# One-hot routing grids: two tokens interleaved instead of four

## The chip, the cores and the metric

The kernel runs on one core of a Trainium2 chip. The core has five engines: TensorE (matrix products, called PE in the profile, with its weight loads listed apart as PEld), VectorE (DVE), ScalarE (ACT), GpSimd (POOL) and SyncE (SP, which here only issues transfers). They run side by side and wait for each other on semaphores. The metric is the time of one execution on the device in microseconds (us). Before the change the median of three runs is 1775.51 us (1775.36 to 1782.84).

## The reference

The kernel computes one layer of a transformer-like backbone for 512 tokens of width 1024: a modulated norm, neighbourhood attention beside a gated MLP, a merge, and then a PEER feed-forward, a product-key lookup of experts. Only the last part matters here:

```
def block(xb):                                   # 128 tokens
    q = (xb @ wq).reshape(128, 8, 2, 128)        # 8 heads, two halves
    s = einsum('thpd,hpkd->thpk', q, sub_keys)
    s_top, i_top = top_k(s, 16)                  # 16 of 128 keys per half
    cand_s = s_top[:, :, 0, :, None] + s_top[:, :, 1, None, :]
    cand_i = i_top[:, :, 0, :, None] * 128 + i_top[:, :, 1, None, :]
    best_s, best_pos = top_k(cand_s, 16)         # 16 experts per head
    experts = take_along_axis(cand_i, best_pos)
    g = softmax(best_s)
    act = gelu(einsum('thkd,td->thk', expert_u[experts], xb))
    return einsum('thk,thkd->td', g * act, expert_v[experts])
```

Each token picks 8 x 16 = 128 of 16384 experts. An expert number is a pair (i, j), each from 0 to 127, and a gate g belongs to it.

## The kernel before, in words

The tokens are four tiles of 128. Three of them (`DT = 3`) take a dense path: all 16384 experts are evaluated as matrix products, in 128 blocks of 128 experts, and the experts that a token did not pick get the weight zero. The fourth tile gathers its experts' rows from memory (L992), on POOL's queue, with its arithmetic on DVE (L1002, L1007).

The dense path has three parts. **The u products** (`dense_u`, lines L82 to L88 and L846): for each of the 128 blocks, `uraw` is loaded, ACT rounds it to `uhi` (L82), DVE takes the rest as `ulo` (L83), PE makes 8 x 3 matmuls of 384 columns (three token tiles wide; L86, L87, L88), and ACT applies the gelu (L846). **The expansion** (L908 to L935): the sparse choice of each token is written out as a full 128 x 128 table of weights. **The v products** (`dense_v`, after L944): the table, read back from memory as `wr`, is multiplied with the gelu of u and gives the left side of the products with the rows of v, 512 columns each.

The change lies in the expansion. For a tile of 128 tokens, `columns` puts the choices on the partitions: `lt[0]` and `lt[1]` hold the row number i and the column number j of choice k (partition) of token t (column), `lt[2]` and `lt[3]` the gate as a large and a small fp16 part. The table of a token is then one product over the 128 choices: a one-hot matrix of j (128 choices x 128 keys), transposed, times a one-hot matrix of i that carries the gate. DVE builds these matrices for eight tokens at a time (`TB = 8`) with four instructions of 1024 fp16 elements per partition: `ea` (L915) and `eb` (L917) compare the numbers with a grid `iot` of 0 to 127, and `oa` (L921, twice) multiplies `ea` with the large and the small part of the gate. PE then makes two accumulating matmuls per token (L926): `eb` of the token is the stationary side, 128 x 128, and `oa` of the token the moving side, 128 columns. ACT copies the tables of four tokens out of PSUM (L927), and every 16 tokens a DMA of 1 MB takes them to memory (L935).

The tokens are not stored one behind the other. The grids have the shape (groups, 128, tokens of a group): neighbouring elements belong to neighbouring tokens, so that DVE's innermost run is over tokens. One token's row of 128 numbers therefore has a step as large as a group, and that is the step at which PE reads both sides of L926.

Per 8 tokens there are so 4 DVE instructions, 16 matmuls and 16 weight loads, 2 ACT copies; 48 such steps make three tiles, so 192 DVE instructions and 768 matmuls in all. The grids have 3 buffers each, the PSUM tiles 4. In the same loop stand the decoding of the next tile's choices (DVE and ACT, `decode`) and every second step one more block of the u products (`more_u`, `UR = 0.5`). The engines' final orders are set before the run by a scheduler, which interleaves these, so that PE goes through 48 of the small matmuls (three steps) in one go and then through some 48 wide ones of u products.

Of the kernel before, what the change touches and what calls it, by code (L numbers as in the profile page):

```python
# [12 lines left out]
HF = mybir.dt.float16  # L13
# [8 lines left out]
P = 128  # L22
# [25 lines left out]
def body(tc, A, out):  # L48
    nc = tc.nc
    pe, dve, act, pool, sp = nc.tensor, nc.vector, nc.scalar, nc.gpsimd, nc.sync  # L50
    es = ExitStack()

    def pool_(stack, name, side="left", bufs=1):
        return stack.enter_context(tc.tile_pool(name=name, bufs=bufs, side=side, reuse_waits="tile"))
# [6 lines left out]
    def ps(tag, shape=(P, 512)):  # L61

        t = psp.tile([P, 512], F32, name="ps" + tag, bufs=4 if tag == "m" else 2)
        n = int(np.prod(shape[1:]))
        v = t[:shape[0], :n]
        if len(shape) == 3:
            v = v.rearrange("p (a b) -> p a b", b=shape[2])
        return v
# [32 lines left out]
    ea = ExitStack()  # L101
# [3 lines left out]
    def t2(dt=F32):  # L105
        return tmp.tile([P, 512], dt, name="t2", bufs=8)
# [165 lines left out]
    eb = ExitStack()  # L272
# [79 lines left out]
    def proj_T(src, g, ins, n=4, sub=None, tags="mmmm"):  # L352

        o = [[ps(t, (P, w)) for t in tags] for _, _, w in ins[:1]]
        for _, _, w in ins[1:]:
            o.append([x[:, i, :] for x in [ps("x", (P, 2, w)) for _ in range(2)] for i in range(2)])
        last = 2 * n - 1
        for c, wh, wl in weights(src, g, n, sub=sub):
            for i, (rh, rl, _) in enumerate(ins):
                for b in range(4):  # L360
                    bs = slice(b * P, (b + 1) * P)
                    if i == 0:
                        mm3(o[i][b], wh[:, bs], wl[:, bs], rh[:, c, :], rl[:, c, :], c == 0, c == last)
                    else:
                        mm3(o[i][b], wh[:, bs], wl[:, bs], rh[:, c, :], rl[:, c, :], c == 0 and b % 2 == 0, c == last and b % 2 == 1, True)
        return o

    def proj_N(src, g, ins):

        o = [ps("m" if i < 4 else "x") for i in range(len(ins))]  # L370
        for c, wh, wl in weights(src, g):
            for i, (lh, ll, t) in enumerate(ins):
                ts = slice(t * P, (t + 1) * P)
                mm3(o[i], lh[:, c, ts], ll[:, c, ts], wh, wl, c == 0, c == 7)
        return o
# [56 lines left out]
    o = proj_N(A["w_in"], 2, lat_N + [(ch, cl, 0), (ch, cl, 1)])  # L432
    for t in range(NT):
        v = t2()
# [22 lines left out]
    for i in range(0, 8, 2):  # L457
        o = ps("xu"[i // 2 % 2], (P, 2, 256))
# [6 lines left out]
    o, = proj_T(A["w_in"], 0, lat_T)  # L465
# [133 lines left out]
    for n in range(2):  # L599
        o, = proj_T(A["w_in"], 7 + n, lat_T, tags=("mmmm", "uuxx")[n])  # L600
# [9 lines left out]
    for n in range(2):  # L610
        for nm, src in (("a", A["w_pa"]), ("b", A["w_pb"])):
            o, = proj_T(src, n, [(*y2[nm], S)], n=2, tags={"a": "mmmm", "b": "uuxx"}[nm])
# [40 lines left out]
    o = proj_N(A["w_out"], 0, [(m_h, m_l, t) for t in range(NT)])  # L653
# [6 lines left out]
    for p in range(2):  # L660
        o = [ps("m"), ps("m")]
# [12 lines left out]
    for p in range(2):  # L674
        if p == 0:
            o = [x[:, i] for x in [ps("x", (P, 2, 256)) for _ in range(2)] for i in range(2)]
        else:
            o = [ps("m", (P, 256)) for _ in range(4)]
# [63 lines left out]
    for g in range(4):  # L742
        if g > 0:
            o, = proj_T(A["wq"], g, [(h2h, h2l, S)], sub=pool)
# [6 lines left out]
        for t in range(NT):  # L751
            o = ps("x" if g < 3 else "m", (P, 4, P))
# [24 lines left out]
    rs = pool_(ro, "rs", "right", bufs=2)  # L777
    TB = 8
    ioa = pr.tile([P, 16, 16], BF, name="ioa")
    iot = rs.tile([P, P, 4], HF, name="iot", bufs=1)  # L780

    def decode(t, res):

# [52 lines left out]
    def more_u(n, sub):  # L836
        for _ in range(n):
            if us_done[0] < P:
                dense_u(us_done[0], sub)
                us_done[0] += 1  # L840
# [16 lines left out]
    def natural_h2():  # L857
        for hf in range(2):
            o = ps("x", (P, 4, P))
            for c in range(4):  # L860
                cc_ = hf * 4 + c
                hs = rs.tile([P, P], F32, name="hs", bufs=1)
                dve.tensor_tensor(hs, f(h2h[:, cc_, GT * P:]), f(h2l[:, cc_, GT * P:]), op=OP.add)
                pe.transpose(o[:, c, :], hs, ident)
            act.activation(h2n[:, hf * 512:(hf + 1) * 512], o.rearrange("p a b -> p (a b)"), AF.Copy)
# [5 lines left out]
    def start_route(t):  # L871
        res = []
        return res, decode(t, res)

    more_u(2, pool)
    pool.iota(ioa, pattern=[[1, 16], [0, 16]], base=0, channel_multiplier=0, allow_small_or_imprecise_dtypes=True)
    pool.iota(iot, pattern=[[1, P], [0, 4]], base=0, channel_multiplier=0, allow_small_or_imprecise_dtypes=True)
    more_u(U0 - 2, pool)
    res, gen = start_route(0)
    for _ in gen:  # L880
# [1 line left out]
    def columns(res):  # L882

        lt = []
        for n, v in enumerate(res):
            o = ps("x", (P, P))
            pe.transpose(o, v.rearrange("p h k -> p (h k)"), ident)
            c = rs.tile([P, P], HF, name="lt%d" % n)
            act.activation(c, o, AF.Copy, scale=1.0 if n < 2 else WS)
            lt.append(c)  # L890

        r = rs.tile([P, P], HF, name="lt3")
        dve.scalar_tensor_tensor(r, o, WS, c, op0=OP.mult, op1=OP.subtract)
        lt.append(r)
        return lt
# [3 lines left out]
    for t in range(DT):  # L899
        lt = lt_next  # L900
        if t == 1:
            natural_h2()
        res, gen = start_route(t + 1)
        for g in range(P // TG):
            stg = rs.tile([P, P, TG], F32, name="stg")
            for u in range(TG // TB):
                t0 = g * TG + u * TB

                def spread(v):

                    return v[:, t0:t0 + TB].rearrange("p (g o t) -> p g o t", g=2, o=1).to_broadcast([P, 2, P, 4])

                grid = iot.rearrange("p (o i) t -> p o i t", o=1).to_broadcast([P, 2, P, 4])
                ea_ = rs.tile([P, 2, P, 4], HF, name="ea", bufs=3)
                dve.tensor_tensor(ea_, spread(lt[0]), grid, op=OP.is_equal)  # L915
                eb_ = rs.tile([P, 2, P, 4], HF, name="eb", bufs=3)
                dve.tensor_tensor(eb_, spread(lt[1]), grid, op=OP.is_equal)  # L917
                oa = []
                for n in range(2):
                    oa.append(rs.tile([P, 2, P, 4], HF, name="oa%d" % n, bufs=3))  # L920
                    dve.tensor_tensor(oa[n], ea_, spread(lt[2 + n]), op=OP.mult)  # L921
                for v in range(2):
                    o = ps("m", (P, 4, P))
                    for x in range(4):
                        for n in range(2):
                            pe.matmul(o[:, x, :], eb_[:, v, :, x], oa[n][:, v, :, x], start=(n == 0), stop=(n == 1))  # L926
                    act.activation(stg[:, :, u * TB + v * 4:u * TB + v * 4 + 4], o.rearrange("p k i -> p i k"), AF.Copy, scale=1.0 / WS)  # L927
                if gen and next(gen, gen) is gen:
                    gen = None
                    if t + 1 < DT:  # L930
                        lt_next = columns(res)
                want_u += UR
                if want_u >= us_done[0] + 1:
                    more_u(1, dve)
            sp.dma_start(wd[t * (P // TG) + g], stg)  # L935
# [219 lines left out]
```

## Time and profile before

| | |
|---|---|
| median of 3 runs | 1775.51 us |
| the profiled execution | 1775.94 us, of which 1774.2 us are its span (first to last instruction) |
| PE busy | 1711.8 us (96%) |
| DVE busy | 1331.5 us (75%) |
| ACT busy | 717.3 us (40%) |
| L926, small matmuls of the expansion | 768 of them, from 654.5 to 880 us of the span |
| share of L926 in the chain that ended last | 5% |

Busy time of PE is the time in which a matmul's record is open; records of neighbours overlap, since a matmul begins before the one ahead has drained. Two different figures of an instruction must be kept apart: how long one lasts (its duration), and how far apart successive ones start (its pace). A group of 32 that is reported as one piece gives the pace.

### The profile page before, as it was taken

The page shows a single profiled execution, that of the slowest core. Times are in us where ns is not written, and L with a number is a line of the kernel's source. Part 1 is how long each engine was busy: PE and PEld are TensorE (multiplying, and loading weights), DVE is VectorE, ACT ScalarE, POOL GpSimd, SP SyncE. Part 2 cuts the span into 40 slices and gives each one's busy share as a digit, 9 for nine tenths or more (in the row PEclk, how much of TensorE's full clock was granted, in tenths as well). Part 3 has the DMA queues.
Part 4 walks back from the last instruction along what each step waited for, and adds up shares of the span by engine and source line. Part 5 has one row for each costly group of instructions (what it writes and reads, how often), then busy time and mean ns, then how long its engine had stood idle before and what let it go on. Part 6 is the DMA issues. An engine that isn't in the chain of part 4 may idle for free.

```text
span 1774.2 us, 24768 instructions
## 1 busy us (share of the span) xinstructions
PE 1711.8 (96%) x9033; PEld 1509.7 (85%) x9033; DVE 1331.5 (75%) x2597; ACT 717.3 (40%) x1106; POOL 540.3 (30%) x383
## 2 busy tenths in 40 slices
PE   7999899999999889999999999999999999999997
PEld 5788678888888779999987888888999999999886
DVE  7677756356679998778567877878777777777786
ACT  5533455533532445545433333333333333333333
POOL 3211420001532320000024544445444444445321
PEclk9999899999999889999999999999999999999999
DMA  8377422233521235565699999989988998998892
GB/s 332 109 244 245 159 90 72 95 112 120 173 72 49 85 120 199 173 213 190 238 328 346 362 334 328 332 325 351 328 303 311 325 316 301 326 314 291 279 324 83
DMA packets 160242, 412.32 MB, mean 232 GB/s; under 512 B 13368, under 2 KB 70712, under 8 KB 156920
## 3 DMA queue, kind: packets, MB, share of 16 engines
q1 hardware_dynamic: 115536, 252.39, 41.1%
q0 software_dynamic: 42480, 154.43, 24.9%
q10 hardware_dynamic: 2104, 3.93, 0.6%
q8 instruction: 70, 1.15, 0.3%
q14 instruction: 52, 0.43, 0.1%
HBM read 375.30 MB, written 35.39 MB: 231 GB/s over the span
## 4 chain that ended last, share of the span: by engine, by line
PE 77%; DVE 12%; DMA 5%; issue 3%; ACT 1%; SPq 0%; POOL 0%; DVEq 0%; POOLq 0%; ACTq 0%
PE psm L86 10%; PE psm L87 10%; PE psm L88 9%; PE psu L86 9%; PE psu L88 9%; PE psu L87 9%; PE psm L926 5%; PE psx L87 4%; PE psx L88 4%; PE psx L86 4%; DMA araw<-in_ada 3%; DMA wgt<-gad 2%; DVE z L705 1%; DVE i L707 1%; DVE i L704 1%
## 5 line engine op out<-in xcount | busy, mean ns | idle before, releaser
L86 PE MATMUL psu<-h2h,uhi 128*128 128x384 f32 x992 | 339.5, 342 | 9.6 <-ACT gsp L846 7.3
L88 PE MATMUL psu<-h2h,ulo 128*128 128x384 f32 x992 | 338.1, 343 | 1.2 <-POOL ulo L83 1.1
L87 PE MATMUL psu<-h2l,uhi 128*128 128x384 f32 x992 | 337.4, 340 | 0.0
L992 POOL DMA_INDIRECT gx<-in_peer_v,ex x128 | 188.2, 1470 | 225.0 <-DVE acc L1007 193.0
L992 POOL DMA_INDIRECT gx<-in_peer_u,ex x128 | 182.6, 1427 | 224.1 <-DVE gj L1002 209.4
L82 ACT ACTIVATE uhi<-uraw 128x1024 fp32r<-128x1024 f32 x126 | 133.6, 1061 | 267.6 <-PE psu L87 239.2
L86 PEld LDWEIGHTS psu<-h2h,uhi 128*128 128x128 f32 x992 | 188.7, 190 | 14.1 <-ACT gsp L846 8.0
L87 PE MATMUL psm<-vlo,wgh 128*128 128x512 f32 x504 | 198.9, 395 | 1.0 <-DVE vlo L83 1.0
L88 PE MATMUL psm<-vhi,wgl 128*128 128x512 f32 x504 | 197.3, 394 | 0.0
L87 PEld LDWEIGHTS psu<-h2l,uhi 128*128 128x128 f32 x992 | 188.2, 190 | 3.9
L88 PEld LDWEIGHTS psu<-h2h,ulo 128*128 128x128 f32 x992 | 188.2, 190 | 3.6 <-POOL ulo L83 2.7
L982 ACT ACTIVATE wgh<-wgt 128x384 fp32r<-128x384 f32 x126 | 65.9, 524 | 297.7 <-issue 192.6
L86 PE MATMUL psm<-vhi,wgh 128*128 128x512 f32 x504 | 174.5, 393 | 5.8 <-ACT wgh L982 5.7
L983 DVE TENSOR_TENSOR wgl<-wgt,wgh 128x384 fp32r<-128x384 f32 x126 | 70.1, 557 | 144.1 <-ACT wgh L982 144.0
L83 DVE TENSOR_TENSOR vlo<-vraw,vhi 128x1024 fp32r<-128x1024 f32 x126 | 154.6, 1227 | 23.4 <-ACT vhi L82 23.4
L83 DVE TENSOR_TENSOR ulo<-uraw,uhi 128x1024 fp32r<-128x1024 f32 x115 | 140.5, 1222 | 39.7 <-ACT uhi L82 39.7
L1007 DVE SCALAR_TENSOR_TENSOR acc<-gx,wg,acc 128x1024 f32<-128x1024 f32 x128 | 163.8, 1279 | 0.0
L1002 DVE SCALAR_TENSOR_TENSOR gj<-gx,h2n 128x1024 bf16<-128x1024 f32 x128 | 155.9, 1218 | 0.0
L82 ACT ACTIVATE vhi<-vraw 128x1024 fp32r<-128x1024 f32 x126 | 131.9, 1047 | 50.8 <-PE psx L88 21.3
L86 PEld LDWEIGHTS psm<-vhi,wgh 128*128 128x128 f32 x504 | 95.3, 189 | 24.6 <-ACT wgh L982 6.7
L87 PEld LDWEIGHTS psm<-vlo,wgh 128*128 128x128 f32 x504 | 95.3, 189 | 20.4 <-DVE vlo L83 1.7
L88 PEld LDWEIGHTS psm<-vhi,wgl 128*128 128x128 f32 x504 | 95.0, 189 | 20.0 <-DVE wgl L983 0.2
(383 smaller groups left out, 3463.7 us busy)
## 6 DMA issues: line engine op xcount, KB each, us to landing
vraw<-in_peer_v SPq DMA_DIRECT2D x126, 512.0 KB, 6.2
uraw<-in_ut SPq DMA_DIRECT2D x124, 512.0 KB, 6.4
wd<-stg SPq DMA_DIRECT2D x24, 1024.0 KB, 4.8
wr<-wd SPq DMA_DIRECT2D x45, 512.0 KB, 7.9
araw<-in_ada POOLq DMA_DIRECT2D x32, 512.0 KB, 5.8
wraw<-in_w_in SPq DMA_DIRECT2D x24, 512.0 KB, 4.1
raw<-in_ada SPq DMA_DIRECT2D x16, 512.0 KB, 8.3
wraw<-in_wq SPq DMA_DIRECT2D x16, 512.0 KB, 3.7
```

The lines of the kernel that those rows point to most:

```text
L82: act.activation(hi, raw, AF.Copy)
L83: return sub.tensor_tensor(lo, raw, f(hi), op=OP.subtract)
L86: pe.matmul(o, lh, rh, start=first, stop=False, skip_group_check=shared)
L87: pe.matmul(o, lh, rl, start=False, stop=False, skip_group_check=shared)
L88: pe.matmul(o, ll, rh, start=False, stop=last, skip_group_check=shared)
L704: dve.max_index(idx[:, 0:8], val[:, 0:8], src)
L926: pe.matmul(o[:, x, :], eb_[:, v, :, x], oa[n][:, v, :, x], start=(n == 0), stop=(n == 1))
L982: act.activation(wh, w, AF.Copy)
L983: last = dve.tensor_tensor(wl, w, f(wh), op=OP.subtract)
L992: pool.indirect_dma_start(out=t, out_offset=None, in_=src, in_offset=bass.IndirectOffsetOnAxis(ap=ex[:, k:k + 1], axis=0))
L1002: dve.scalar_tensor_tensor(junk, u, 1.0, h2n, op0=OP.mult, op1=OP.mult, accum_out=actg[:, i:i + 1])
L1007: dve.scalar_tensor_tensor(acc, v, wg[:, i:i + 1], acc, op0=OP.mult, op1=OP.add)
```

## The change

The grids get the shape (4 groups, 128, 2 tokens) in place of (2 groups, 128, 4 tokens). The number of elements, of instructions and their operations stay, and so does the place in PSUM where each token's table lands. What differs is the step at which DVE's operands and PE's operands are read and written: PE's two sides of L926 had a step of four fp16 elements and now have two, and DVE's innermost run over tokens had four elements and now has two. The grid `iot` of 0 to 127 is half as large.

```
-    iot = rs.tile([P, P, 4], HF, name="iot", bufs=1)
+    iot = rs.tile([P, P, 2], HF, name="iot", bufs=1)
...
-    pool.iota(iot, pattern=[[1, P], [0, 4]], ...)
+    pool.iota(iot, pattern=[[1, P], [0, 2]], ...)
...
-    return v[:, t0:t0 + TB].rearrange("p (g o t) -> p g o t", g=2, o=1).to_broadcast([P, 2, P, 4])
-grid = iot.rearrange("p (o i) t -> p o i t", o=1).to_broadcast([P, 2, P, 4])
-ea_ = rs.tile([P, 2, P, 4], HF, name="ea", bufs=3)
+    return v[:, t0:t0 + TB].rearrange("p (g o t) -> p g o t", g=4, o=1).to_broadcast([P, 4, P, 2])
+grid = iot.rearrange("p (o i) t -> p o i t", o=1).to_broadcast([P, 4, P, 2])
+ea_ = rs.tile([P, 4, P, 2], HF, name="ea", bufs=3)
 dve.tensor_tensor(ea_, spread(lt[0]), grid, op=OP.is_equal)
...
-            pe.matmul(o[:, x, :], eb_[:, v, :, x], oa[n][:, v, :, x], start=(n == 0), stop=(n == 1))
+            pe.matmul(o[:, x, :], eb_[:, 2 * v + x // 2, :, x % 2], oa[n][:, 2 * v + x // 2, :, x % 2], start=(n == 0), stop=(n == 1))
```

(`eb` and the two `oa` change their shapes as `ea` does.) No instruction changes its place: on PE, DVE, ACT and SP the rows are the same, one for one. On POOL one instruction, the one that fills the grid `iot`, is smaller:

```order
@@ -55,5 +55,5 @@
 L876 IOTA ioa 128x256
 L83 TENSOR_TENSOR ulo<-uraw,uhi 128x1024 x2
-L877 IOTA iot 128x512
+L877 IOTA iot 128x256
 L83 TENSOR_TENSOR ulo<-uraw,uhi 128x1024 x9
 L957 DMA wr<-wd 128x8x128 x3
```

It stands where it stood, ahead of nine instructions for u blocks.

## Rows read from the trace of the kernel before

**Rows 1.** The page: span and busy time of each engine.
```profile
span 1774.2 us, 24768 instructions
PE 1711.8 (96%) x9033; PEld 1509.7 (85%) x9033; DVE 1331.5 (75%) x2597; ACT 717.3 (40%) x1106; POOL 540.3 (30%) x383
```
**Rows 2.** Windows of the expansion: stretch, length, busy of each engine, PEclk, DMA share, GB/s.
```profile
654.50:700.00 45.50, 45.50 (x318) 44.10 (x318) 40.37 (x68) 24.01 (x36) 0.00 (x0) 1.00 0.51 176
700.00:780.00 80.00, 79.42 (x546) 76.31 (x544) 63.77 (x108) 43.53 (x65) 0.00 (x0) 1.00 0.57 197
780.00:860.00 80.00, 80.00 (x549) 77.15 (x547) 62.46 (x93) 38.47 (x60) 0.00 (x0) 1.00 0.59 201
860.00:880.50 20.50, 20.50 (x140) 19.82 (x139) 9.50 (x16) 8.81 (x14) 1.83 (x2) 1.00 0.80 268
```
**Rows 3.** Windows of all that follows the expansion, same columns.
```profile
882.50:1774.20 891.70, 874.03 (x4244) 776.59 (x4242) 686.31 (x883) 315.42 (x448) 383.24 (x264) 0.99 0.89 310
```
**Rows 4.** The chain that ended last, around 840 us: start, us, what.
```profile
837.75 3.79 PE psm L926 x32
...
842.25 1.91 PE psm L926 x16
...
852.12 3.78 PE psm L926 x32
```
**Rows 5.** Waits from 635 to 882 us: total, times, longest.
```profile
DVE ulo L83 <- ACT uhi L82: 24.4, 16, 6.3
DVE eb L917 <- PE psm L926: 17.8, 21, 1.8
```
**Rows 6.** Line L926: durations in ns, min/median/max.
```profile
L926 PEld LDWEIGHTS <-eb x768: 112/117/137, 654.5 to 879.7; 128*128 128x128 f16 x192
L926 PE MATMUL psm<-oa,eb x768: 273/297/304, 654.5 to 879.9; 128*128 128x128 f16 x192
```
**Rows 7.** Other matmuls by width: two lines' instructions, and a group of the page.
```profile
L166 PE MATMUL psx<-hi,s x64: 274/278/562, 9.2 to 71.0; 128*4 128x256 f32 x64
...
L86 PE MATMUL psu<-h2h,uhi x258: 332/337/443, 654.0 to 881.6; 128*128 128x384 f32 x129
...
L87 PE MATMUL psm<-vlo,wgh 128*128 128x512 f32 x504 | 198.9, 395 | 1.0 <-DVE vlo L83 1.0
```
**Rows 8.** Timeline, PE: start us, us; 256 columns, then 384 columns.
```profile
40.88 0.28 PE L166 MATMUL psx<-hi,s 128*4 128x256 f32 x1
...
41.58 0.28 PE L166 MATMUL psx<-hi,s 128*4 128x256 f32 x1
...
833.95 0.33 PE L86 MATMUL psu<-h2h,uhi 128*128 128x384 f32 x1
...
834.47 0.34 PE L86 MATMUL psu<-h2h,uhi 128*128 128x384 f32 x1
```
**Rows 9.** Timeline, PEld: the first weight load of a burst, and the first two.
```profile
654.49 0.11 PEld L926 LDWEIGHTS <-eb 128*128 128x128 f16 x1 [0.16 <-DVE oa L921]
...
654.49 0.15 PEld L926 LDWEIGHTS <-eb 128*128 128x128 f16 x2 [0.16 <-DVE oa L921]
```
**Rows 10.** DVE instructions of the stage: durations in ns, min/median/max.
```profile
L921 DVE TENSOR_TENSOR oa<-ea,lt x96: 676/683/687, 650.8 to 869.5; 128x1024 f16<-128x1024 f16 x96
...
L818 DVE TENSOR_TENSOR eq<-pf,ioa x8: 1197/1218/1222, 613.0 to 833.2; 128x2048 bf16<-128x2048 bf16 x8
...
L83 DVE TENSOR_TENSOR ulo<-uraw,uhi x33: 1210/1220/1227, 655.5 to 877.0; 128x1024 fp32r<-128x1024 f32 x33
```
**Rows 11.** Windows of line L926 alone: stretch, length, PE and PEld busy with counts.
```profile
654.50:700.00 45.50, 21.28 (x170) 18.88 (x171) 1.00 0.51 176
700.00:780.00 80.00, 34.38 (x270) 29.53 (x268) 1.00 0.57 197
780.00:860.00 80.00, 34.30 (x270) 29.33 (x267) 1.00 0.59 201
860.00:880.50 20.50, 8.23 (x64) 7.00 (x64) 1.00 0.80 268
```

More of the change, by code (lines that the diff above doesn't have):

```diff
@@ L876, in body @@
     pool.iota(ioa, pattern=[[1, 16], [0, 16]], base=0, channel_multiplier=0, allow_small_or_imprecise_dtypes=True)
-    pool.iota(iot, pattern=[[1, P], [0, 4]], base=0, channel_multiplier=0, allow_small_or_imprecise_dtypes=True)
+    pool.iota(iot, pattern=[[1, P], [0, 2]], base=0, channel_multiplier=0, allow_small_or_imprecise_dtypes=True)
     more_u(U0 - 2, pool)
@@ L909, in spread @@
                 def spread(v):
-                    return v[:, t0:t0 + TB].rearrange("p (g o t) -> p g o t", g=2, o=1).to_broadcast([P, 2, P, 4])
-                grid = iot.rearrange("p (o i) t -> p o i t", o=1).to_broadcast([P, 2, P, 4])
-                ea_ = rs.tile([P, 2, P, 4], HF, name="ea", bufs=3)
+                    return v[:, t0:t0 + TB].rearrange("p (g o t) -> p g o t", g=4, o=1).to_broadcast([P, 4, P, 2])
+                grid = iot.rearrange("p (o i) t -> p o i t", o=1).to_broadcast([P, 4, P, 2])
+                ea_ = rs.tile([P, 4, P, 2], HF, name="ea", bufs=3)
                 dve.tensor_tensor(ea_, spread(lt[0]), grid, op=OP.is_equal)
-                eb_ = rs.tile([P, 2, P, 4], HF, name="eb", bufs=3)
+                eb_ = rs.tile([P, 4, P, 2], HF, name="eb", bufs=3)
                 dve.tensor_tensor(eb_, spread(lt[1]), grid, op=OP.is_equal)
@@ L919, in body @@
                 for n in range(2):
-                    oa.append(rs.tile([P, 2, P, 4], HF, name="oa%d" % n, bufs=3))
+                    oa.append(rs.tile([P, 4, P, 2], HF, name="oa%d" % n, bufs=3))
                     dve.tensor_tensor(oa[n], ea_, spread(lt[2 + n]), op=OP.mult)
```

## The prediction

> **What bounds the kernel now.** I read the busy shares first. PE is busy 96% of the span, DVE 75% [rows 1], so PE is the first suspect; but a share over the whole span says nothing about the stage that the change touches, so the windows come next. [...] Behind the expansion PE is busy 874 of 892 us [rows 3]: what comes later waits for PE too and none of its PE work is touched, so I take every microsecond won or lost in the expansion as one won or lost at the end.
>
> The chain of waits shows the same from the other side: it runs through L926 in pieces of 32 and 16 matmuls, with u products between them [rows 4]. One period, from one piece of 32 to the next, is 852.12 - 837.75 = 14.4 us, of which 3.79 + 1.91 = 5.7 us are the small matmuls. The waits say what DVE's idle time is made of: it waited 17.8 us for L926 to give a buffer of `eb` free, and 24.4 us for ACT's `uhi` [rows 5], which in turn stands behind the u products.
>
> **How fast the small matmuls go, and why.** 32 of them in 3.79 us is a pace of 118 ns for 128 columns [rows 4]. Wide matmuls of contiguous fp32 are the measure: 256 columns follow each other at (41.58 - 40.88) / 6 = 117 ns, 384 columns at (834.47 - 833.95) / 3 = 173 ns [rows 8], so 128 columns more cost 57 ns. A matmul of 128 columns with that rate would have a pace of 117 - 57 = 60 ns; L926 needs twice that. Its duration says so too: 297 ns (273 at least), against 278 for 256 columns, 337 for 384 and 395 for 512 [rows 6, 7]. At about 58 ns per 128 columns, 128 contiguous ones would take some 220 ns. L926 therefore behaves in pace and in duration like a matmul with twice its columns.
>
> It could be the weight load in front of each matmul rather than the stream. A load lasts 117 ns [rows 6], as long as the pace, which looks like a cause. But the first two loads of a burst end only 0.15 - 0.11 = 0.04 us apart [rows 9], so most of a load's duration is delay and not occupation, and a slow load would not lengthen the matmul's own duration. I hold the moving side's reads to be the limit: eight bytes lie between neighbouring elements of `oa`, four between those of the fp32 operands that stream at full rate. The change makes it four bytes on both sides.
>
> **The change part by part.**
>
> PE: 768 matmuls and 768 loads, as many as before. Bounds of the new pace: 60 ns (the full rate, from the two widths) and 118 ns (nothing gained). I take 65 ns, near the lower end, since the step in bytes becomes that of the full-rate rows, with a little left for the weight load, whose 40 ns must fit beside it. The cut is 768 x (118 - 65) = 40.7 us of PE's time.
>
> What lies beside other work: DVE. Its instructions stay in number. Where DVE's work exceeds what PE has left, DVE sets the length. By stretch, with the counts of L926 [rows 11] and the busy times [rows 2]:
> - 654.5 to 700: PE 45.5 - 170 x 0.053 = 36.5; DVE 40.4. DVE is longer; at most 5.1 us are won.
> - 700 to 780: 270 x 0.053 = 14.3 off; PE 65.1, DVE 63.8. 14.3 won at most.
> - 780 to 860: 14.3 off again; PE 65.7, DVE 62.5. 14.3 won at most.
> - 860 to 880.5: 64 x 0.053 = 3.4 off; DVE only 9.5. 3.4 won.
>
> Together 37.1 us if both engines ran without a gap. They can't: DVE would be 95 to 98% busy in the middle stretches, it runs in order, and its grids have three buffers, just the three steps that PE takes in one burst. DVE now idles 17.8 + 24.4 = 42.2 us in waits that PE is behind [rows 5]. I let a quarter of these remain, about 10 us, which gives 37 - 10 = 27 us. So the cover that hides DVE now, PE's slowness, is used up by the change, and DVE's work is what is late next.
>
> DVE: the same four instructions per step, now with innermost runs of two. No row shows a run of two. Runs of four cost 683 ns for 1024 fp16 elements and runs of sixteen 1218 ns for 2048 [rows 10]; these fit one straight line of about 0.52 ns per element plus 150 ns, so shorter runs have cost nothing so far. From below I see no gain, since these are already at the 2-byte rate. From above the bound is the fp32 row, 1220 ns for 1024 elements [rows 10], if pairs were no longer taken together: 537 ns more for each of 192. I take nothing, as the row nearest to it (runs of four) is on the line; the upper end is a rival below.
>
> ACT and POOL: L927 reads the same PSUM places; the smaller grid is filled once, before the stage. Both nothing, and their slack (ACT is busy about half of the stage [rows 2]) would hide more than that. DMA is at 0.51 to 0.80 of its share in the stage; the same bytes in 27 us less make it some 12% denser, still below full. The stage behind starts with 0.89 and keeps its own length.
>
> Sum: the profiled execution took 1775.94 us, 1.7 us around its span of 1774.2; it is within 0.5 us of the median of the runs. 1775.9 - 27 = 1749 us.
>
> [...]
>
> **Rivals.**
>
> First, PE gains, but DVE takes most of it. For it: DVE's 80 to 89% [rows 2], and that all three buffers of a burst are freed within some 3 us. Against it: DVE's own work of 176 us (the sum of its four stretches) leaves 50 us of the stage. If half or more of the 42 us of waits stays, the gain is 37 - 21 = 16 us and less: 1757 to 1767 us.
>
> Second, no change: the step of four is not what slows L926. For it: the load's duration of 117 ns equals the pace [rows 4, 6]; if a load can begin only when the matmul ahead begins, and the next matmul must wait for its end, then the pace is the load's and doesn't move. Against it are the two loads that end 0.04 us apart [rows 9], and the matmul's long duration. A few nanoseconds less, 118 to 110, would be 768 x 0.008 = 6 us: 1770 to 1779 us.
>
> Third, slower: DVE loses its rate on runs of two. For it: no row has them, and the grids are the one place where DVE goes through rows so short. Against it: runs of four and sixteen are on one line [rows 10]. At the fp32 rate DVE's work in the stage is 176 + 192 x 0.537 = 279 us, more than the stage's 226 us: 53 us slower, 1829 us. It decides from where DVE's work passes 226 us, which is 50 / 192 = 0.26 us more per instruction, or about 0.2 us with the waits that stay.
>
> **How the numbers follow.** The forecast, 1737 to 1758 us (a pace between 60 and 80 ns, and a loss to waits between none and 15 us), gets 0.57. DVE taking most of it gets 0.14, no change 0.21, slower 0.08. About 0.5% or 9 us is what a measurement of this kernel can tell from no change. Faster is then 0.57 + 0.14 = 0.71, the same 0.21, slower 0.08. The range from 1735 us (a pace of 60 ns cuts 44.5 us, some 41 of which could land) to 1778 us takes in the first three but the edge, and leaves out the slower case.
>
> **What would show it.** Right: L926 in the chain goes from 3.8 us per 32 to some 2.1 us, its duration falls from 297 to 220 to 250 ns, PE falls below 95% in the expansion while DVE rises above 90%, `eb` waits less for L926, PE waits for `oa` or `ea`, and DVE's durations stay at 683 ns. Wrong: L926 keeps 118 ns (the second rival), or DVE's instructions get longer than 0.7 us (the third), or PE's cut is there and the end doesn't come sooner because the stage behind, with DMA at 0.89, starts late for another reason.

## The result and the profile after

The changed kernel takes 1735.96 us (median of 4 runs, 1733.37 to 1738.93) against 1775.43 us: a ratio of 0.9768, 95% interval 0.9752 to 0.9784. It is 39.5 us faster; the forecast was 27 us. The direction holds, and so does what the forecast said of PE's reads; what it said of DVE's part does not. The time lies at the very edge of the range of 1735 to 1778 us, by the ratio (0.9768 x 1775.43 = 1734 us) just outside it.

The page of the changed kernel answers to [rows 1]:

```profile
span 1737.2 us, 24768 instructions
PE 1673.4 (96%) x9033; PEld 1472.1 (85%) x9033; DVE 1328.5 (76%) x2597; ACT 708.2 (41%) x1106; POOL 541.6 (31%) x383
```

PE's busy time fell by 38 us, DVE's by 3: DVE does what it did, PE needs less. Line L926 (durations in ns, min/median/max, then first and last start in us) answers to [rows 6], and the DVE lines under it to [rows 10]:

```profile
L926 PEld LDWEIGHTS <-eb x768: 96/97/103, 657.7 to 842.0; 128*128 128x128 f16 x192
L926 PE MATMUL psm<-oa,eb x768: 217/218/236, 657.7 to 842.1; 128*128 128x128 f16 x192
...
L917 DVE TENSOR_TENSOR eb<-lt,iot x48: 677/682/692, 651.9 to 833.7; 128x1024 f16<-128x1024 f16 x48
...
L921 DVE TENSOR_TENSOR oa<-ea,lt x96: 677/682/686, 653.9 to 835.1; 128x1024 f16<-128x1024 f16 x96
```

A matmul lasts 218 ns, the 220 that wide contiguous ones pointed to, in place of 297. The runs of two cost DVE nothing (682 ns). From the first to the last start of L926 there are 842.1 - 657.7 = 184.4 us, before 879.9 - 654.5 = 225.4 [rows 6]: 41.0 us less. The chain of waits, in order of time, answers to [rows 4] (start, us, what):

```profile
809.04 1.85 PE psm L926 x32
...
811.64 0.94 PE psm L926 x16
...
820.75 1.85 PE psm L926 x32
```

32 matmuls take 1.85 us, a pace of 58 ns with the entry into the piece, where it was 118; the period is 820.75 - 809.04 = 11.7 us, before 14.4. Of the waits (total, times, longest) those of DVE shrank [rows 5]; first from 657 to 780 us, then from 780 to 845:

```profile
DVE ulo L83 <- ACT uhi L82: 3.5, 4, 2.1
...
DVE ulo L83 <- ACT uhi L82: 9.6, 4, 3.7
```

DVE no longer waits for L926 at all, and in the first two thirds hardly for `uhi`. The windows (columns as in [rows 2]) show that PE is still busy nearly throughout, that DVE now is too until 820 us, and that what follows kept its length [rows 3]:

```profile
660.00:700.00 40.00, 40.00 (x338) 38.88 (x337) 40.00 (x71) 22.62 (x39) 0.00 (x0) 1.00 0.70 244
700.00:740.00 40.00, 38.36 (x316) 36.50 (x315) 38.26 (x68) 24.56 (x41) 0.00 (x0) 0.96 0.59 214
740.00:780.00 40.00, 40.00 (x328) 38.97 (x326) 36.73 (x57) 21.88 (x37) 0.00 (x0) 1.00 0.73 259
780.00:820.00 40.00, 40.00 (x333) 38.35 (x332) 40.00 (x61) 21.84 (x35) 0.00 (x0) 1.00 0.67 239
820.00:845.00 25.00, 25.00 (x218) 24.12 (x217) 15.40 (x26) 13.94 (x24) 1.84 (x2) 1.00 0.80 274
...
842.00:1737.00 895.00, 877.55 (x4262) 780.46 (x4259) 686.31 (x883) 317.48 (x450) 384.23 (x264) 0.99 0.89 311
```

DVE, the third busy time, is busy 92 to 100% until 820 us. Two busy engines don't tell which one sets the length. Since PE's order is the same in both kernels, its work can be cut at the same instructions as in [rows 2] (the same numbers of matmuls, but for one), and then each stretch has a length before and after:

```profile
657.75:693.38 35.63, 35.63 (x318) 34.52 (x318) 35.63 (x61) 21.29 (x36) 0.00 (x0) 1.00 0.63 224
693.38:760.77 67.39, 65.75 (x546) 63.15 (x544) 64.85 (x112) 40.44 (x67) 0.00 (x0) 0.97 0.64 226
760.77:825.91 65.14, 65.14 (x550) 62.72 (x547) 62.20 (x96) 35.78 (x61) 0.00 (x0) 1.00 0.69 245
825.91:842.71 16.80, 16.80 (x140) 16.23 (x140) 9.84 (x17) 8.06 (x14) 1.84 (x2) 1.00 0.89 310
```

The lengths are 35.6, 67.4, 65.1 and 16.8 us; before they were 45.5, 80, 80 and 20.5. Only the second holds idle time of PE, 1.6 us at 716 to 718 us, in two waits for ACT; right behind them the granted clock is 0.50 for 3.4 us. And the chain that ended last has no piece of DVE from 657 to 842 us (the longer one of the two waits, a window, and the chain's shares):

```profile
717.35 0.44 PE L86 MATMUL psu<-h2h,uhi 128*128 128x384 f32 x1 [1.36 <-ACT gact L846]
...
719.10:722.50 3.40, 3.40 (x13) 3.40 (x12) 3.40 (x8) 0.97 (x1) 0.00 (x0) 0.50 1.00 319
...
by line: PE psu L88 24.4%; PE psu L86 24.1%; PE psu L87 23.7%; PE psm L926 23.4%; ACT stg L927 0.8%; issue 0.8%; ACT L793 0.7%; ACT L846 0.7%; ACT uhi L82 0.6%; PE psx L864 0.4%; PE psx L887 0.4%; ACT G L793 0.2%; ACT gact L846 0.0%
```

Of the 41.0 us, 37.0 arrive in the profiled span (1774.2 to 1737.2): the expansion began 657.7 - 654.5 = 3.2 us later, and the rest is 0.8 us longer. The later start isn't the change's doing: a line far ahead of it, where both kernels are the same, begins anywhere in a range of 4 us in different executions. Here it is in the changed kernel and then in the third experiment below:

```profile
L754 PE MATMUL psx<-keys,t x96: 270/275/275, 498.1 to 557.6; 128*128 128x128 f32 x96
```
```profile
L754 PE MATMUL psx<-keys,t x96: 270/275/275, 494.0 to 553.4; 128*128 128x128 f32 x96
```

### The profile page after: what moved, and what is told of

Same layout as the page of the kernel before. It is cut to its first block, busy times and chain, and to the rows that moved or that the text cites. A ratio compares the mean times of both kernels' runs of the same rounds, so it can differ in the third digit from the quotient of the medians.

```text
span 1737.2 us, 24768 instructions
## 1 busy us (share of the span) xinstructions
PE 1673.4 (96%) x9033; PEld 1472.1 (85%) x9033; DVE 1328.5 (76%) x2597; ACT 708.2 (41%) x1106; POOL 541.6 (31%) x383
## 4 chain that ended last, share of the span: by engine, by line
PE 76%; DVE 14%; DMA 6%; issue 3%; ACT 1%; POOL 0%; SPq 0%; DVEq 0%; POOLq 0%; ACTq 0%
PE psm L86 10%; PE psm L87 10%; PE psu L86 10%; PE psu L88 10%; PE psm L88 10%; PE psu L87 10%; PE psx L87 4%; PE psx L88 4%; PE psx L86 4%; DMA araw<-in_ada 3%; PE psm L926 2%; DVE z L705 1%; DMA wgt<-gad 1%; DVE i L707 1%; DVE i L704 1%
## 5 line engine op out<-in xcount | busy, mean ns | idle before, releaser
L983 DVE TENSOR_TENSOR wgl<-wgt,wgh 128x384 fp32r<-128x384 f32 x126 | 70.1, 557 | 145.2 <-ACT wgh L982 144.4
```

The source lines that it names most:

```text
L983: last = dve.tensor_tensor(wl, w, f(wh), op=OP.subtract)
```

## The experiments

All are variants of the changed kernel. In the first four each side of L926 has its own number of interleaved tokens, `TA` for `ea` and `oa`, `TBI` for `eb`; in the changed kernel both are 2, before both were 4.

**One side at a time.** The first run has `TA, TBI = 2, 4`:

```
 ea_ = rs.tile([P, TB // TA, P, TA], HF, name="ea", bufs=3)
 eb_ = rs.tile([P, TB // TBI, P, TBI], HF, name="eb", bufs=3)
...
 pe.matmul(o[:, x, :], eb_[:, (4 * v + x) // TBI, :, (4 * v + x) % TBI],
           oa[n][:, (4 * v + x) // TA, :, (4 * v + x) % TA], ...)
```

> Only the moving side (oa, and ea with it) has a step of two; the weights (eb) keep a step of four. My theory (the moving side's reads are what made L926 slow): the pace falls from 118 to about 57 ns per matmul and the duration from 297 to about 218 ns, as with both sides at two, the time is 1733 to 1742 us. Its first rival (the weight load at a step of four sets the pace): pace stays near 118 ns, time 1770 to 1780 us. A second one (both sides count): pace between, 85 to 100 ns, time 1750 to 1765 us.

```profile
L926 PEld LDWEIGHTS <-eb x768: 110/113/138, 656.7 to 841.9; 128*128 128x128 f16 x192
L926 PE MATMUL psm<-oa,eb x768: 217/221/254, 656.7 to 842.0; 128*128 128x128 f16 x192
...
703.46 1.94 PE psm L926 x32
```

1737.09 us, ratio 0.9788 (0.9763 to 0.9813): the moving side alone gives the whole gain. 32 matmuls take 1.94 us, 61 ns each (58 with both). The load still lasts 113 ns, almost twice the pace: its duration did not limit the pace, and the second rival falls.

The mirror image, `TA, TBI = 4, 2`:

> The mirror image: only the weights (eb) have a step of two, the moving side (ea, oa) keeps four. My theory: pace and duration of L926 stay at 118 and 297 ns, only the weight load's own duration falls from 117 to about 97 ns, time 1770 to 1780 us. The rival (weights set the pace): pace about 57 ns, time 1733 to 1742 us. Both sides count: 85 to 100 ns, 1750 to 1765 us.

```profile
L926 PEld LDWEIGHTS <-eb x768: 96/115/119, 657.6 to 881.5; 128*128 128x128 f16 x192
L926 PE MATMUL psm<-oa,eb x768: 275/296/301, 657.6 to 881.7; 128*128 128x128 f16 x192
...
700.06 3.74 PE psm L926 x32
```

1775.44 us, ratio 0.9992 (0.9977 to 1.0007): nothing. One detail of the expectation missed: the load's median is 115 ns and not 97, though its operand has the smaller step; only the shortest last 96. Behind the slow matmuls (296 ns) the record of a load with the same step is longer than behind the fast ones (115 against 97 ns), so that it can't be read as the load's own cost.

**Other steps.** No interleaving, `TA, TBI = 1, 1`:

> No interleaving: both sides of L926 have a step of one. [...] For DVE the innermost element is now one number spread along 128, so ea, eb and oa read one operand with a step of zero: if that costs DVE its 2-byte rate, the four instructions last about 1220 ns, DVE gets 192 x 0.54 = 103 us more and the time is 1780 to 1840 us; if not, they stay at 682 ns and the time is as with a step of two, 1733 to 1742 us.

```profile
L926 PE MATMUL psm<-oa,eb x768: 216/219/314, 656.4 to 933.3; 128*128 128x128 f16 x192
...
L921 DVE TENSOR_TENSOR oa<-ea,lt x96: 1208/1212/1218, 654.2 to 930.7; 128x1024 f16<-128x1024 f16 x96
...
700.00:780.00 80.00, 67.57 (x483) 62.48 (x483) 80.00 (x93) 35.32 (x57) 0.00 (x0) 0.93 0.50 177
```

1827.08 us, ratio 1.0286 (1.0267 to 1.0305). PE gains nothing further (219 ns; 56 ns from start to start within a piece), while DVE's instructions go from 682 to 1212 ns, where one operand is now one number repeated in place of a run of different ones. DVE is busy for all of its 80 us there. So the interleaving is what DVE needs, and two tokens are enough for it. The scheduler's order is another one here (55 more matmuls of u products lie in the stage). The expansion is 933.3 - 656.4 = 276.9 us long, practically DVE's own work: the 176 us before plus 192 x (1.212 - 0.683) = 102 us make 278. That is also the price I had put on the third rival (1829 us), here by another cause than runs of two.

Eight tokens, `TA, TBI = 8, 8`:

> Eight tokens interleaved: both sides of L926 have a step of eight elements, 16 bytes. If the reads cost in proportion to the bytes between elements (57 ns at two, 118 at four), the pace is about 237 ns: 768 x 0.119 = 91 us more than with four, time 1855 to 1880 us. If a step of four already is the worst (one element per access, whatever lies between), the pace stays at 118 ns and the time at 1770 to 1780 us. DVE's durations stay at 683 ns in both.

```profile
L926 PE MATMUL psm<-oa,eb x768: 392/413/450, 655.9 to 1001.7; 128*128 128x128 f16 x192
...
720.97 7.53 PE psm L926 x32
...
700.00:780.00 80.00, 80.00 (x358) 62.85 (x357) 42.29 (x71) 31.05 (x45) 0.00 (x0) 0.76 0.36 126
```

A pace of 7.53 / 32 = 235 ns, as the reading by bytes has it: 16 bytes between elements 235, 8 bytes 118, 4 bytes 58, and no less at 2. But the time is 1897.72 us (ratio 1.0684, 1.066 to 1.0708), 18 us above the upper end of the expected 1855 to 1880. The granted clock tells why: 0.76 in this window where before it was 1.00 [rows 2]. Two neighbouring windows, the first from within a burst of 32 slow matmuls on, with 16 more of them behind it, the second with wide matmuls and then the start of the next burst; and two of the wide matmuls, one at either level:

```profile
683.30:693.50 10.20, 10.20 (x41) 7.76 (x40) 5.34 (x10) 2.56 (x5) 0.00 (x0) 0.50 0.63 217
693.60:703.70 10.10, 10.10 (x54) 8.55 (x53) 6.47 (x10) 3.48 (x5) 0.00 (x0) 1.00 0.29 94
...
692.63 0.52 PE L86 MATMUL psu<-h2h,uhi 128*128 128x384 f32 x1
...
694.05 0.34 PE L86 MATMUL psu<-h2h,uhi 128*128 128x384 f32 x1
```

At 0.50 a wide matmul lasts 520 ns, at 1.00 it lasts 340. The slow matmuls themselves don't feel the clock; 14 of them at 1.00 and 16 at 0.50 (two windows, and a piece in each):

```profile
883.20:886.60 3.40, 3.40 (x17) 2.26 (x17) 2.02 (x4) 0.60 (x1) 0.00 (x0) 1.00 0.24 99
708.00:711.90 3.90, 3.90 (x18) 2.60 (x18) 0.79 (x3) 0.69 (x3) 0.00 (x0) 0.50 0.80 260
...
708.09 3.76 PE psm L926 x16
...
883.27 3.31 PE psm L926 x14
```

Their paces are 236 and 235 ns: it is the step that sets them, and not TensorE's clock. All engines' orders are those of the kernel before, so the step alone makes the difference. The reads at 16 bytes cost twice: their own time (235 ns a matmul), and the clock of the wide matmuls among and behind them (0.50).

**Is DVE the bound now, and do the engines lose time to each other?** The next four were run beside each other, the first unaltered.

> The changed kernel once more, unaltered, for the next three to be compared with on the same chip. Theory: the expansion's length is, stretch by stretch, the longer one of PE's and DVE's work, with nothing lost between them: about 184 us from the first to the last L926, wherever it starts; time 1733 to 1740 us. The rival, the term of my prediction by which about 10 us of waits remain, would have 194 us there.

1736.64 us, ratio 0.9757 (0.9736 to 0.9779). L926 goes from 657.3 to 841.8 us, 184.5 us, as in the first trace of the changed kernel and ten less than the rival has. That speaks against the waits, but it repeats the length that the theory was made from, and "stretch by stretch" isn't borne out: cut at the same instructions as above, the stretches are 35.8, 67.4, 65.1 and 16.8 us here, while the longer engine would need 40.4, 63.8, 63.5 and 16.6.

Two buffers in place of three:

```
-ea_ = rs.tile([P, 4, P, 2], HF, name="ea", bufs=3)
+ea_ = rs.tile([P, 4, P, 2], HF, name="ea", bufs=2)     # eb and both oa alike
```

> The grids ea, eb and oa have two buffers in place of three. If engines that take turns on few buffers lose time in waits, as I assumed, this shows it: the three steps of one burst of 48 no longer fit, and the expansion is 8 to 20 us longer, 1743 to 1757 us, with waits of DVE for L926. If the waits are free as long as each engine's work is there, the length stays within 4 us of the one with three.

1740.01 us, ratio 0.9767 (0.9744 to 0.9791), no difference from three buffers. The scheduler answered with another order (29 more matmuls of u products lie in the stage, which is 187.4 us long), so it isn't a test of the buffers in the old order; it does show that two buffers do as well in an order made for two.

DVE relieved, by leaving one instruction per step out:

```
-for n in range(2):
+for n in range(1):
     oa.append(rs.tile([P, 4, P, 2], HF, name="oa%d" % n, bufs=3))
-    dve.tensor_tensor(oa[n], ea_, spread(lt[2 + n]), op=OP.mult)
+    dve.tensor_tensor(oa[n], ea_, spread(lt[2 + n]), op=OP.mult); oa.append(oa[0])
```

> The second multiplication of each step (L921 for the small part of the gate) is left out and the large part's grid is used for both products, so the gate's small part isn't computed; PE's work is the same. DVE has 48 x 0.6 = 29 us less, spread over the expansion. Theory: DVE bounds only its first part, so 4 to 8 us are won and then PE bounds all of it, about 177 us: 1728 to 1733 us. If DVE bounds it throughout, 15 to 29 us are won (1707 to 1721 us). If DVE is no bound at all, nothing is won.

1726.44 us, ratio 0.9695 (0.9676 to 0.9715), 10 us less than the unaltered one: a little more than the theory's 4 to 8, far from the 15 to 29 of a DVE that bounds throughout. It doesn't show that DVE is the bound, since here too the order changed: 207 matmuls of u products, 207 x 0.175 = 36.2 us of PE's time, moved behind the expansion. The trace says where the 10 us arise. The expansion is 144.4 us long, with the 36.2 us 180.6 in place of 184.4: some 4 us, as PE's idle time and the stretch at half clock are gone from it. What lies behind is 924.6 us long, without the 36.2 us 888.4 in place of 895.1: some 7 us, as PE's idle time there falls from 17.7 to 14.2 us and the time at half clock in its first 100 us from 10.2 to 3.4 us. Whether the lighter DVE or the new order took the 4 us, this run doesn't separate.

A way to relieve DVE without leaving work out: half of its subtractions in the first two tiles to POOL.

```
-more_u(1, dve)
+more_u(1, pool if t < 2 and us_done[0] % 2 else dve)
```

> Eight of the u blocks in the first two tiles have their subtraction (L83) on POOL, which idles there, in place of DVE. If DVE bounds the first stretches, it has 8 x 1.14 = 9 us less there, and the expansion is shorter by 3 to 6 us (down to PE's own work, some 178 us): 1728 to 1734 us. If DVE isn't the bound, or POOL's 2.6 us per subtraction holds PE's u products up, no change or 1 to 5 us more.

```profile
L83 POOL TENSOR_TENSOR ulo<-uraw,uhi x10: 2384/3851/15267, 638.6 to 761.7; 128x1024 fp32r<-128x1024 f32 x10
...
678.68 15.28 POOL ulo L83
...
PE psu L88 <- POOL ulo L83: 17.6, 4, 9.6
```

1762.55 us, ratio 0.9903 (0.9884 to 0.9921): 26 us slower than the unaltered one, worse than either theory said. (The order changed here too: 62 of the u products' matmuls moved behind the expansion, which is 196.7 us long.) The same subtraction that takes POOL 2.4 us at best takes up to 15.3 us while DVE works through the grids, and PE waits for it (the last row, from 635 to 860 us). During the longest one DVE ran without a gap from 676 to 692 us, and it ended 2 us behind that.

**More or fewer u blocks in the expansion**, `UR = 0.3` and `UR = 0.65` for 0.5:

> The changed kernel with fewer u blocks called for between the steps of the expansion (UR = 0.3 in place of 0.5; the scheduler decides where they end up). With the faster matmuls PE and DVE have nearly the same work in the expansion. If DVE is the bound of its first part and PE has gaps of some 6 us just behind it, moving blocks behind shortens the first and fills the second: 3 to 8 us won, 1729 to 1734 us. If both are as well balanced as the stretches say, no more than 3 us either way: 1734 to 1740 us.

> The opposite: more u blocks in the expansion (UR = 0.65). PE gets more work where DVE already limits or nearly does, and fewer blocks are left to fill the gaps behind: 0 to 8 us lost, 1737 to 1745 us; if the balance doesn't matter, 1734 to 1740 us.

1737.70 us, ratio 0.9766 (0.975 to 0.9783), and 1737.96 us, ratio 0.9773 (0.9759 to 0.9787). Neither is a test of more or fewer blocks. With 0.3 the scheduler put out the order of the changed kernel again: PE, DVE, ACT and POOL go through the same instructions, one for one. With 0.65 seven places in PE's order and two in DVE's differ, and the 759 matmuls of u products among the small ones stay. So the two are further runs of the changed kernel, or nearly so, and both expectations stay open. No version that computes everything beat the changed kernel.

## Why the prediction was right and where it was wrong

**The cause** was right: L926 behaved like a matmul of twice its columns because of the moving side's step. The two kernels with one side each show it, and they refute the rival of the weight load. The paces are the firmer evidence, 118 against 58 ns, as they come from the starts of the records; a matmul's end is modelled in the profile, and so is its duration. That the distance in bytes counts, and not in elements, is less firm: fp16 at a step of two and contiguous fp32, both four bytes, run at the same rate (58 and 57 ns per 128 columns), but no run has fp32 at a wider step.

**DVE's runs of two at no cost** was right (682 ns), though the argument for it was weak: runs of four and of sixteen lie on one line as any two points do. That pairs are taken together was my reading of the two rates: the runs show 682 ns with an interleave of two and 1212 without one, and not how they come about. The stage behind follows unchanged, as forecast (895.1 us from the last L926 to the end; before 1774.2 - 879.9 = 894.3).

**The pace** was mis-sized: I took 65 ns, with 60 as the lower bound; it is 57 to 58. The 60 kept the 3 ns by which 117 exceeds twice 57, and the small matmuls show nothing of them; nor was the margin for the weight load needed. The forecast's other edge, 80 ns, no run shows either: with a moving step of two elements they took 58 (both sides) and 61 (the moving side alone). The term still came out near. Only 723 of the 768 follow another small matmul. From start to start these took 85.33 us before and 42.47 after, 42.9 us less (added up from the starts in the two traces), against 768 x 0.053 = 40.7: too little per matmul, too many matmuls.

**The step that failed** is what DVE was to take back: in the first stretch "DVE is longer; at most 5.1 us are won", and on top of it "I let a quarter of these remain, about 10 us"; together 40.7 - 27 = 13.7 us. It took nothing that the traces show. PE went through the first stretch in 35.6 us, where DVE's work was 40.4, and DVE did 61 of its former 68 instructions in that time without PE waiting for it. In the kernel before DVE stood ahead of PE as far as its buffers let it, which is what its 17.8 us of waits for L926 were [rows 5]; so it could fall back. Its waits were a reserve, and I counted them as a loss to come. Behind the 13.1 us that remain PE doesn't wait for `ulo`. The signs that I named for it did not come either: PE stayed busy for 183.3 of 185.0 us in place of falling below 95%, and its weight loads waited 1.1 us in all for `oa` and `ea`.

What PE did lose is about 2 us of the 42.9. It sat idle 1.6 us at 716 to 718 us, 0.6 in the kernel before, behind ACT, which loads its function table for the exponential of the softmax (L793) and then again for the gelu (L846), 1.28 us each. In the 3.4 us at half clock behind that, ten wide matmuls came 320 ns apart in place of 175, which is 1.5 us. I had put ACT at nothing, by its slack.

That the longer engine of each stretch gives the right total is luck. With 57 ns, so 61 off each, PE has 45.5 - 10.4 = 35.1, then 62.9, 63.5 and 16.6 us, and the longer engine of each 40.4 (DVE) + 63.8 (DVE) + 63.5 (PE) + 16.6 (PE) = 184.3 us, against 184.4 measured; but the first stretch was 4.8 us shorter than that, the second 3.6 and the third 1.6 longer. Over the whole stage the comparison holds: DVE's work of 176 us is below PE's, and PE set the length, as it did before (idle for 0.6 of 226 us [rows 2]); without interleaving DVE's 278 us are far above it, and DVE did (276.9).

So the expansion got 42.9 - 2 = 41 us shorter, of which 37.0 are in the profiled span and 39.5 in the medians. The range's lower end rested on the 60 ns and on DVE's part of the first stretch, and came out too high. That three buffers are scarce was a wrong worry as well.

**The first rival**, that DVE takes most of the gain, did not come about: all but some 2 us of PE's gain arrived, and those went to ACT and the clock.

## What to carry to other kernels

Compare a slow matmul's duration and pace with those of contiguous ones of other widths: if it lasts like one of twice its columns, look at how many bytes lie between the elements of its moving side (here 297 ns at 8 bytes, 218 at 4). When an edit makes the bounding engine faster, sum up over the whole stage what each engine still has to do and take the longer one: an engine that runs ahead on its buffers may have more work in one stretch than the other without holding it up (here 40.4 us of DVE's in a stretch that PE went through in 35.6). Subtract something for waits only with a row that shows the engine waiting that will be the longer one. Before you read a run as a test, see that its engines' orders differ as you meant. Choose a layout's interleave as the smallest that keeps VectorE at its rate, here two (682 ns for 1024 elements, 1212 without interleaving).

## What the runs showed of the hardware that was not expected

- TensorE's moving reads went by the distance between elements: 128 fp16 columns took 56 to 58 ns at 2 and 4 bytes, 118 at 8, 235 at 16, the last at either level of the clock. A stationary side at 8 in place of 4 bytes moved the pace by 3 ns (61 against 58).
- With the slowest of these reads the granted clock fell to 0.50 in stretches of some 10 us, in which PE was busy without a gap (10.20 of 10.20 us), and a wide matmul went from 340 to 520 ns.
- A GpSimd subtraction of 128 x 1024 fp32 took from 2.4 to 15.3 us beside VectorE's fp16 stream; what holds it up there no run here shows.
